# A hybrid decoder step on one core: its scales in column pieces, x transposed raw and kept for the residual

## The chip, the core and the metric

The kernel runs on one core of a Trainium2 chip. Its engines work side by side, each through its own instruction stream: TensorE (PE in the profile, its weight loads PEld), VectorE (DVE), ScalarE (ACT), GpSimd (POOL) and SyncE (SP), which here only issues transfers to the DMA engines. Matmuls write to PSUM (eight banks of 512 floats in each of 128 partitions), everything else lives in SBUF. The metric is the device time of one execution in microseconds (us).

## The reference

One inference step of a one-layer decoder trunk for a prompt of 512 positions and for 8 samples of one position, width 1024, float32. Cut to what the change touches:

```python
cs = jax.nn.silu(c)
mod = cs @ w_mod + b_mod
sh1, sc1, g1, sh2, sc2, g2 = jnp.split(mod, 6, axis=-1)
h = _rmsnorm(x, norm1_g) * (1.0 + sc1) + sh1
u = h @ w_in
qa, fa, ia, oga, xb, yb, ga, gb = _split_cols(u)
...
x = x + g1 * (merged @ w_out)
h2 = _rmsnorm(x, norm2_g) * (1.0 + sc2) + sh2
x = x + g2 * (jnp.square(jax.nn.relu(h2 @ w_ff1)) @ w_ff2)
y = _rmsnorm(x, final_norm_g)
```

Between the two parts stand a gated linear recurrence over eight heads (states, outputs) and a convolution with a second recurrence. `_rmsnorm` divides by the root of the mean square of a row of x.

## The kernel before, in words

All activations are kept transposed: 128 channels on the partitions, the 512 positions of the prompt and the 8 samples in the free dimension (T = 520, in two halves of 260). A product with a weight tile of 1024 x 128 goes over eight k blocks of 128 channels. For precision every weight tile and every activation is split into a high and a low part (`hi`, `lo`, type fp32r), so that one k block takes six matmuls of 260 columns: high with high, high with low, low with high, each for two halves. Weight tiles come through a pool of four buffers (`wst`); ACT makes their high parts, DVE their low parts. Outside the start, `gemm` (line 156) runs these products; their matmuls stand under L151.

**The start** (`begin`) prepares h and makes the first three products (the f, q and output-gate columns of head 0) by hand. There, PE, ACT and DVE instructions run in the order in which the code writes them: `InOrder` chains each instruction to the one before it on its engine. That helper is line 69, so all of them stand under L69 and are told apart by their tiles. In the order of before:

- SP loads the conditioning vectors, x in four tiles of 128 positions (`xn`), one weight tile, the eight row blocks of `w_mod` for the scales (part 1; 128 x 1024 each, tile `wm`), and three weight tiles; later eight row blocks for the shifts (part 0), and further weight tiles.
- ACT sums squares of x, DVE makes the inverse roots (`rs_y`), and ACT and DVE multiply x by them row by row, while positions are still on the partitions.
- PE multiplies the conditioning by the row blocks (`mod_rows`, tile `pt`) and between them transposes the normed x, block by block; ACT and DVE copy the blocks back (`put_back`).
- When all eight row blocks are through, `mod_out` copies the sums out (`modev`), and `mod_cols` transposes them into columns and adds bias and gain: `modT`, the scales.
- `scaled(k)`: ACT writes the high part of block k of x times its scale, DVE the low part. `products(n, ks)` makes tile n's products over blocks ks. The weight tiles' parts are `fhi` and `flo`.
- The products run without the shift. The shift rows follow; `mod_cols(0, ...)` gives `shp`. The shift's share in the first three products is added by matmuls of the shift with the raw weights (tile `pw`, then `shwh`, `shwl`) and an indicator of positions (`ind`). `again(k)` rewrites block k of h with the shift (ACT high part, DVE `ht` and low part, POOL the samples) for all later products.
- `masks_of`, `bounds`, `exponentials`, `indicator`, `decays` prepare small constants of the recurrences, mostly on DVE.

Behind the start come the heads, gates and branches, then **`load_xT`** (line 927): it reads x a second time, transposes it in 32 blocks through PSUM (`xin` to `pb`), with eight small transposes for the samples, and has ACT copy it into eight slots `ma`. These are the residual that `out_proj` adds to. The rest (the MLP in a Strassen-like scheme, the last norm) is not touched. The order outside the start is made by a scheduler from the dependencies and priorities.

Of the kernel before, what the change touches and what calls it, by code (L numbers as in the profile page):

```python
# [6 lines left out]
F32 = mybir.dt.float32  # L7
# [10 lines left out]
NB = 8  # L18
# [58 lines left out]
class Kernel:  # L77
# [204 lines left out]
    def bounds(self, r):  # L282

        nc = self.nc
        pl = self.hc.tile([128, 16], F32, name="pl")
        self.transpose_in(pl, r, 16)
# [45 lines left out]

    def parameters_mod_in(self, r):
        pm = self.consts.tile([128, 64], F32, name="pm")
        self.transpose_in(pm, r, 64)
        self.bmod, self.n1g, self.n2g = pm[:, 0:48], pm[:, 48:56], pm[:, 56:64]
        for part in (1, 4):
            c = self.bmod[:, part * 8:part * 8 + 8]
            self.nc.vector.tensor_scalar(c, c, 1.0, None, OP.add)
# [64 lines left out]
    def load_rows(self, part, k, t=None):  # L404

        t = t or self.start.tile([128, D], F32, name="wm", bufs=NWM)
        self.nc.sync.dma_start(t, self.i["w_mod"][0, k * 128:(k + 1) * 128, part * D:(part + 1) * D])
        return t

# [51 lines left out]
    def norm_samples(self):  # L461
        nc = self.nc
        j = self.pmm.tile([128, 2, 512], F32, name="mm").rearrange("p a b -> p (a b)")
        nc.vector.tensor_tensor(j[:NB], self.xsn, self.xsn, OP.mult)
        nc.vector.tensor_reduce(self.ss1[:NB, NC:NC + 1], j[:NB], mybir.AxisListType.X, OP.add)

    def norm_x(self):
        nc, ss = self.nc, self.ss1
        for t in range(NC):
            j = self.pmm.tile([128, 2, 512], F32, name="mm").rearrange("p a b -> p (a b)")  # L470
            last = nc.scalar.activation(j, self.xn[:, t], AF.Square, accum_out=ss[:, t:t + 1])
        ss = ss[:, 0:8]
        nc.vector.tensor_scalar(ss, ss, 1.0 / D, EPS, OP.mult, OP.add)
        self.rs1 = self.rsqrt_small(ss, 8)
        return last

    def scale_x(self):
        nc, ss = self.nc, self.rs1
        for t in range(NC):
            x = self.xn[:, t]  # L480
            if t % 2:
                nc.scalar.activation(x, x, AF.Copy, scale=ss[:, t:t + 1])
            else:
                nc.vector.tensor_scalar(x, x, ss[:, t:t + 1], None, OP.mult)
        nc.vector.tensor_scalar(self.xsn, self.xsn, ss[:NB, NC:NC + 1], None, OP.mult)

    def xcols(self, k, n=1):
        return self.xn[:, :, k * 128:(k + n) * 128]

    def transposed(self, k, n, ps):  # L490

        for j in range(n):
            x = self.xcols(k + j)
            for t in range(NC):
                self.nc.tensor.transpose(ps[:, j, t * 128:(t + 1) * 128], x[:, t], self.ident)
        return k, n, ps

    def put_back(self, copy, t):
        k, n, ps = t
        copy(self.xcols(k, n).rearrange("p t (j f) -> p j t f", j=n), ps.rearrange("p j (t f) -> p j t f", t=NC))  # L500

    def transposed_s(self):
        nc = self.nc
        ps = self.pps.tile([128, 512], F32, name="ps")
        for k in range(KO):
            nc.tensor.transpose(ps[:, k * NB:(k + 1) * NB], self.xsn[:, k * 128:(k + 1) * 128], self.ident[:NB, :NB])
        xs = self.start.tile([128, KO, NB], F32, name="xhs")
        nc.vector.tensor_copy(xs, ps[:, :KO * NB].rearrange("p (k b) -> p k b", b=NB))
        return xs

    def scaled(self, k, shift=False):


        nc = self.nc
        sc, sh = self.modc(1, k)[:, 0:1], self.shp[:, k, 0:1]
        v = lambda t: t[:, :L].rearrange("p (t f) -> p t f", f=128)
        (hi, lo), x = self.h[k], self.xcols(k)
        if not shift:
            nc.scalar.activation(v(hi), x, AF.Copy, scale=sc)
            return lambda: nc.vector.scalar_tensor_tensor(v(lo), x, sc, v(hi).bitcast(F32), OP.mult, OP.subtract)  # L520
        f = self.start.tile([128, L], F32, name="ht", bufs=2)
        self.start_act = nc.scalar.activation(v(hi), x, AF.Identity, bias=sh, scale=sc)
        nc.vector.tensor_scalar(v(f), x, sc, sh, OP.mult, OP.add)
# [403 lines left out]
    def load_xT(self):  # L927

        nc, i = self.nc, self.i
        xs = self.tail.tile([16, D], F32, name="rows", bufs=1)[:NB]  # L930
        nc.gpsimd.dma_start(xs, i["x_sample"][:, 0])
        pt = self.ppt.tile([128, 512], F32, name="pt")
        for k in range(KO):
            nc.tensor.transpose(pt[:, k * NB:(k + 1) * NB], xs[:, k * 128:(k + 1) * 128], self.ident[:NB, :NB])
        xst = self.tail.tile([128, KO * NB], F32, name="xst", bufs=1)
        nc.vector.tensor_copy(xst, pt[:, :KO * NB])
        self.x = []
        for m in range(KO):
            t4 = self.tail.tile([128, NC, 128], F32, name="xin", bufs=2)
            nc.gpsimd.dma_start(t4, i["x_prompt"][0].rearrange("(t p) f -> p t f", p=128)[:, :, m * 128:(m + 1) * 128])  # L940
            ps = self.ppb.tile([128, 512], F32, name="pb")
            for c in range(NC):
                nc.tensor.transpose(ps[:, c * 128:(c + 1) * 128], t4[:, c], self.ident)
            x = self.slot(self.ma, "ma")
            nc.scalar.copy(x[:, :L], ps)
            nc.vector.tensor_copy(x[:, L:], xst[:, m * NB:(m + 1) * NB])
            self.x.append(x)
# [617 lines left out]
    def run(self):  # L1565
# [17 lines left out]
        self.hlast = self.hc.tile([128, KO, 9], F32, name="hlast")  # L1583
        self.oaT_d = self.dram.tile([H, 128, L], F32, name="oaT_d")
# [67 lines left out]
    def begin(self):  # L1652
# [6 lines left out]
        ps = lambda: self.pps.tile([128, 512], F32, name="ps")  # L1659
        self.load_c()  # L1660
        self.identity()
        rb, rm, par = self.load_bounds(), self.parameters_mod(), self.parameters()
        rows = [self.start.tile([128, D], F32, name="wm", bufs=NWM) for _ in range(KO)]
        self.load_x()
        keys = [self.head_cols(0)[j] for j in (0, 1, 3)]
        raw = [self._load_w(keys[0], self.wst)]
        rows = [self.load_rows(1, k, t) for k, t in enumerate(rows)]
        raw += [self._load_w(key, self.wst) for key in keys[1:]]
# [11 lines left out]
        def samples(shift):  # L1680
# [3 lines left out]
            else:  # L1684
                q.tensor_tensor(fs, xs, self.modT[:, 8:16, 1:9], OP.mult)
                parts(slice(0, KO))
# [9 lines left out]
        self.norm_samples()  # L1696
        self.bounds(rb)
        self.parameters_mod_in(rm)
        self.masks_of(4)
        last = self.norm_x()  # L1700
        self.exponentials()
# [194 lines left out]
```

## Time and profile before

| what | value |
|---|---|
| median of 3 runs | 1022.83 us (1021.65 to 1023.39) |
| the profiled execution's own time | 1022.73 us |
| its span, first to last instruction | 1020.9 us |
| PE, DVE, ACT busy | 98%, 66%, 50% of the span |
| mean granted PE clock | 0.995 |
| HBM read, written | 123.61 MB, 11.26 MB |

The profile is of one execution. A row of the timeline gives the start in us, the busy time, the engine, the line, the operation, output and inputs, the shape and how many instructions were merged; in brackets the engine's idle time before it and what ended that. A row of a tile's view gives the least, median and greatest duration in ns. A row of the groups gives the busy time in us, the mean duration in ns, and the idle time before. A fp32 matmul leaves two records, so `x16` in the trace can be eight matmuls.

### The profile page before, as it was taken

The page shows a single profiled execution, that of the slowest core. Times are in us where ns is not written, and L with a number is a line of the kernel's source. Part 1 is how long each engine was busy: PE and PEld are TensorE (multiplying, and loading weights), DVE is VectorE, ACT ScalarE, POOL GpSimd, SP SyncE. Part 2 cuts the span into 40 slices and gives each one's busy share as a digit, 9 for nine tenths or more (in the row PEclk, how much of TensorE's full clock was granted, in tenths as well). Part 3 has the DMA queues.
Part 4 walks back from the last instruction along what each step waited for, and adds up shares of the span by engine and source line. Part 5 has one row for each costly group of instructions (what it writes and reads, how often), then busy time and mean ns, then how long its engine had stood idle before and what let it go on. Part 6 is the DMA issues. An engine that isn't in the chain of part 4 may idle for free. (4 is left out here: it accounts for less than half of the span.)

```text
span 1020.9 us, 23540 instructions
## 1 busy us (share of the span) xinstructions
PE 996.0 (98%) x9756; PEld 966.2 (95%) x9756; DVE 673.5 (66%) x1412; ACT 514.0 (50%) x964; POOL 123.9 (12%) x229
## 2 busy tenths in 40 slices
PE   5999999999999999999999999999999999999997
PEld 3899999999999989998999999999999999999997
DVE  6776867786596667345233557677766776777685
ACT  4555735645573564334211235466555655646663
POOL 3210000000000001001010001021321231242150
PEclk9999999999999999999999999999999999999998
DMA  9673353434335335239656677331672483273242
GB/s 322 220 210 109 107 169 102 122 117 143 114 108 157 115 108 168 76 116 298 195 163 191 201 218 217 85 99 46 149 182 64 97 194 104 53 170 89 63 83 84
DMA packets 201821, 143.67 MB, mean 141 GB/s; under 512 B 6766, under 2 KB 189702, under 8 KB 201706
## 3 DMA queue, kind: packets, MB, share of 16 engines
q1 hardware_dynamic: 191090, 128.08, 42.1%
q0 software_dynamic: 10608, 14.05, 7.1%
q8 instruction: 76, 1.25, 0.5%
q14 instruction: 31, 0.25, 0.1%
q10 hardware_dynamic: 16, 0.03, 0.0%
HBM read 123.61 MB, written 11.26 MB: 132 GB/s over the span
## 5 line engine op out<-in xcount | busy, mean ns | idle before, releaser
L151 PE MATMUL mm<-h,whi 128*128 128x260 f32 (+1 forms) x2944 | 488.8, 285 | 0.0
L151 PEld LDWEIGHTS mm<-h,whi 128*128 128x128 f32 x2944 | 409.7, 189 | 3.3 <-issue 2.5
L151 PE MATMUL mm<-h,wlo 128*128 128x260 f32 x1472 | 303.5, 285 | 0.0
L112 ACT CAST whi<-wst 128x1024 fp32r<-128x1024 f32 x164 | 171.8, 1049 | 229.8 <-PE mm L151 178.9
L115 DVE TENSOR_TENSOR wlo<-wst,whi 128x1024 fp32r<-128x1024 f32 x164 | 200.3, 1222 | 125.6 <-ACT whi L112 124.2
L151 PEld LDWEIGHTS mm<-h,wlo 128*128 128x128 f32 x1472 | 230.5, 189 | 0.8 <-issue 0.4
L151 PE MATMUL mm<-a,whi 128*128 128x260 f32 x512 | 84.0, 284 | 0.0
L151 PEld LDWEIGHTS mm<-a,whi 128*128 128x128 f32 x512 | 70.3, 188 | 1.7 <-ACT whi L112 1.2
L151 PE MATMUL mm<-a,wlo 128*128 128x260 f32 x256 | 52.2, 284 | 0.0
L893 POOL DMA_DIRECT2D t<-obT_d x8 | 4.4, 550 | 392.5 <-PE pb L798 302.6
L1286 DVE TENSOR_TENSOR f<-f 128x260 f32<-128x260 f32 x64 | 27.4, 427 | 27.6 <-ACT f L1281 26.9
L1275 ACT ACTIVATE ft<-ft,fsh 128x512 f32<-128x512 f32 (+2 forms) x36 | 24.0, 675 | 36.1 <-DVE ft L1272 36.1
L151 PE MATMUL mm<-b,whi 128*128 128x260 f32 x256 | 41.6, 285 | 0.0
L1278 POOL TENSOR_TENSOR ft<-ft,fsh 128x8 f32<-128x8 f32 x28 | 18.4, 658 | 186.9 <-DVE ft L1272 186.9
L151 PEld LDWEIGHTS mm<-a,wlo 128*128 128x128 f32 x256 | 39.6, 188 | 0.0
L151 PEld LDWEIGHTS mm<-b,whi 128*128 128x128 f32 x256 | 35.0, 188 | 2.1 <-ACT whi L112 1.2
L682 DVE TENSOR_TENSOR X<-X,tb 128x512 f32<-128x512 f32 x48 | 31.0, 687 | 3.2 <-PE ps L674 1.9
L1320 POOL DMA_DIRECT2D ma<-snap x28 | 28.0, 1014 | 35.8 <-issue 27.2
L1302 POOL DMA_DIRECT2D ma<-snap x28 | 26.0, 927 | 40.1 <-DMA ma<-snap 28.2
L1281 ACT ACTIVATE f<-ft 128x520 f32<-128x520 f32 (+1 forms) x36 | 20.8, 587 | 15.0 <-POOL ft L1279 13.0
L175 ACT ACTIVATE gate<-pb,pa 128x260 f32<-128x260 f32 x32 | 15.4, 482 | 21.0 <-PE pb L798 21.0
L151 PE MATMUL mm<-b,wlo 128*128 128x260 f32 x128 | 25.8, 283 | 0.0
(573 smaller groups left out, 1867.9 us busy)
## 6 DMA issues: line engine op xcount, KB each, us to landing
wst<-in_w_in_dram SPq DMA_DIRECT2D x64, 512.0 KB, 4.2
wst<-in_w_mod_dram SPq DMA_DIRECT2D x32, 512.0 KB, 4.6
wst<-in_w_ff_dram SPq DMA_DIRECT2D x64, 256.0 KB, 3.7
wst<-in_w_ff_dram SPq DMA_DIRECT2D x32, 512.0 KB, 4.6
wm<-in_w_mod_dram SPq DMA_DIRECT2D x16, 512.0 KB, 10.5
st<-in_state_hgrn_dram SPq DMA_DIRECT2D x8, 512.0 KB, 5.1
vb<-vd SPq DMA_DIRECT2D x8, 512.0 KB, 3.7
out_dram<-st SPq DMA_DIRECT2D x8, 512.0 KB, 3.5
```

The source lines that it names most:

```text
L112: ins = self.nc.scalar.copy(hi, st)
L115: self.nc.vector.tensor_tensor(lo, st, hi.bitcast(F32), OP.subtract)
L151: self.last_product = self.nc.tensor.matmul(ps[s][:, :c.stop - c.start], x, y[:, c], start=first and n == 0, stop=last and n == 2)
L175: ins = self.nc.scalar.activation(out, x, AF.Sigmoid, **kw)
L682: nc.vector.tensor_tensor(half, half, factors(tbs, x, b), OP.mult)
L893: nc.gpsimd.dma_start(t, self.obT_d[n])
L1275: nc.scalar.activation(t[:, :p], t[:, :p], AF.Relu, bias=sh[:, 0:1])
L1278: eng.tensor_tensor(t[:, p:], t[:, p:], sh[:, 1:9], OP.add)
L1281: nc.scalar.activation(f, self.two(self.ft)[:, a:a + n], AF.Square)
L1286: self.nc.vector.tensor_tensor(f[:, n], f[:, a], f[:, b], op)
L1302: nc.gpsimd.dma_start(x[1][:, b], v[:, :n], accum_op=OP.add)
L1320: nc.gpsimd.dma_start(x[t][:, a], s[p], accum_op=OP.add)
```

## The change

- **Scales in pieces of columns.** Instead of eight row blocks, `w_mod`'s part 1 is loaded as four pieces of 256 columns over all 1024 rows (1 MB each), each behind one of the first weight tiles. `piece` multiplies one piece by the conditioning, all eight k at once; `piece_cols` turns it into the scales of two blocks k. The shift rows come as four loads of two row blocks.
- **x transposed raw.** As each tile of x lands, PE transposes it into all eight PSUM banks; DVE and ACT copy halves into eight tiles `xT` (slots `ma`).
- **The factors per block.** `spread_root` writes the inverse roots on the diagonal of four matrices (`rsd`), and a product with ones spreads them over all partitions (`spread`, tile `pb`). `rooted(k)` on DVE multiplies block k of `xT` by it. The multiplication row by row and `put_back` are gone.
- **Stored for the residual.** POOL adds the samples to `xT`, SP stores the eight tiles to DRAM (`xT_d`), and `load_xT` becomes eight loads.
- **Another order.** Products run for pairs of blocks behind their piece; `bounds`, the masks 4, 8 and 16 and the parameters go behind the first pairs; `again` is called for six blocks, not three, ahead of the matmuls of the shift; the shift is added at the very end.

```diff
+        for n in range(4):
+            if n < FIRSTS:
+                raw.append(self._load_w(keys[n], self.wst))
+            w = self.start.tile([128, KO, 256], F32, name="wm", bufs=4)
+            c = D + 256 * n
+            nc.sync.dma_start(w, self.i["w_mod"][0, :, c:c + 256].rearrange("(k p) n -> p k n", p=128))
+            pieces.append(w)
...
+    def spread_root(self, ps, ps_s):
+        nc, rs, eye = self.nc, self.rs1, self.ident
+        one = self.ones_r.bitcast(F32)
+        d = self.start.tile([128, NC, 128], F32, name="rsd")
         for t in range(NC):
+            nc.vector.tensor_scalar(d[:, t], eye, rs[:, t:t + 1], None, OP.mult)
...
+    def piece(self, i, w):
+        nc = self.nc
+        pt = self.ppt.tile([128, 512], F32, name="pt")
         for k in range(KO):
+            j = 32 * (k % 4)
+            nc.tensor.matmul(pt[j:j + 32, :256], self.cT[:, k, :], w[:, k, :], start=k < 4, stop=k >= 4)
+        return i, pt, self.mod_out(pt)
...
+        for t in range(NC):
+            for k in range(KO):
+                nc.tensor.transpose(banks[k][:, t * 128:(t + 1) * 128], self.xn[:, t, k * 128:(k + 1) * 128], self.ident)
+            nc.scalar.activation(junk[:, t * D:(t + 1) * D], self.xn[:, t], AF.Square, accum_out=self.ss1[:, t:t + 1])
+            if t == 1:
+                half(dve, 0, *range(KO))
+        half(dve, 1, 5)
+        half(act, 1, 4, 6, 0)
+        self.norm_root()
...
+        p = self.piece(0, pieces[0])
+        spread = pb()
+        self.spread_root(spread, pr)
...
+        self.piece_cols(p)
...
+        rooted = lambda k: nc.vector.tensor_tensor(self.xr[:, k], self.xT[k][:, :L], spread, OP.mult)
+        rooted(0)
...
+        products(0, 0, 1)
+        half(act, 1, 2, 3)
+        for k in range(KO):
+            plain.sync.dma_start(self.xT_d[k], self.xT[k])
         split_first(1)
+        p = self.piece(1, pieces[1])
         split_rest(1)
...
         products(1, 0, 1)
+        self.piece_cols(p)
+        for k in (2, 3):
+            rooted(k)
+            self.scaled(k)()
+        samples(False, slice(2, 4))
         split_first(2)
+        products(0, 2, 3)
+        p = self.piece(2, pieces[2])
+        products(1, 2, 3)
+        self.piece_cols(p)
         split_rest(2)
+        for k in (4, 5):
+            rooted(k)
             self.scaled(k)()
...
+        dve(pl, ppl[:, :16])
+        self.parameters_in(*par)
+        p = self.piece(3, pieces[3])
+        self.first.append([ps()[:, :HALF], ps()[:, :HALF]])
...
+        products(2, 0, 1, 2, 3)
+        self.piece_cols(p)
...
-        again(0, 1, 2)
-        products(0, 6)
-        products(1, 6)
+        again(*range(0, 6))
...
     def load_xT(self):
-        xs = self.tail.tile([16, D], F32, name="rows", bufs=1)[:NB]
-        nc.gpsimd.dma_start(xs, i["x_sample"][:, 0])
...
+        self.x = [self.slot(self.ma, "ma") for _ in range(KO)]
+        for m, x in enumerate(self.x):
+            self.nc.gpsimd.dma_start(x, self.xT_d[m])
```

**PE, from the scales to the products of the first tiles.** Names: `pt<-wm,cT` is the conditioning times a part of `w_mod`, `pt<-pick,modev` and `pb<-ident,modev` make the columns, `mm<-h,fhi` and `mm<-h,flo` are products, `xn` is x before the transposition. Before:

```order
L69 MATMUL pt<-wm,cT 32x256 x12
L69 MATMUL ps<-ident,rb 128x57
L69 MATMUL ps<-ident,rc 128x64
L69 MATMUL ps<-ident,rd 128x96 x2
L69 MATMUL pb<-ident,modev 128x36 x2
L69 MATMUL ps<-ident,xn 128x128 x8
L69 MATMUL mm<-h,fhi 128x260 x4
L69 MATMUL mm<-h,flo 128x260 x2
```

Now, the same place in the changed program:

```order
L69 MATMUL pt<-pick,modev 128x9 x2
L69 MATMUL mm<-h,fhi 128x260 x8
L69 MATMUL mm<-h,flo 128x260 x4
L69 MATMUL pt<-wm,cT 32x256 x8
L69 MATMUL mm<-h,fhi 128x260 x8
L69 MATMUL mm<-h,flo 128x260 x4
L69 MATMUL pt<-pick,modev 128x9 x2
L69 MATMUL mm<-h,fhi 128x260 x8
L69 MATMUL mm<-h,flo 128x260 x4
L69 MATMUL pt<-wm,cT 32x256 x8
```

The columns were made once, ahead of all products; now they are made four times, and each time behind the products of the pair before.

**DVE, from one pair of blocks to the next in the changed program.** `xn<-ma,pb` is `rooted`, `modT` the scales, `h<-xn,modT,h` a low part of h, `flo` one of a weight tile, `pl` and `pa` copies of parameters. Before, the low parts stood in one run:

```order
L69 TENSOR_TENSOR modT<-modT,pm 128x2x4x9
L69 SCALAR_TENSOR_TENSOR h<-xn,modT,h 128x512 x2
L69 TENSOR_TENSOR flo<-wst,fhi 128x1024
L69 SCALAR_TENSOR_TENSOR h<-xn,modT,h 128x512
L69 TENSOR_TENSOR flo<-wst,fhi 128x1024
L69 SCALAR_TENSOR_TENSOR h<-xn,modT,h 128x512 x5
```

Now, for the blocks 4 and 5:

```order
L69 TENSOR_TENSOR modT<-pt,pm 128x18
L69 TENSOR_TENSOR modT<-modT,pm 128x18
L69 TENSOR_TENSOR flo<-wst,fhi 128x1024
L69 TENSOR_TENSOR xn<-ma,pb 128x512
L69 SCALAR_TENSOR_TENSOR h<-xn,modT,h 128x512
L69 TENSOR_TENSOR xn<-ma,pb 128x512
L69 SCALAR_TENSOR_TENSOR h<-xn,modT,h 128x512
L69 COPY pl<-ps 128x16
L69 COPY pa<-ps 128x313
```

The first `modT` reads the columns that PE makes; each `rooted` stands directly ahead of the low part of the same block, and the copies of the parameters stand behind both.

**DVE, around the low part of the shift's weights (`shwl`).** `shp` are the shift columns, each pair of `ht` and `h<-ht,h` is one `again`. Before:

```order
L69 TENSOR_TENSOR shp<-pb,pm 128x2x4x9
L69 TENSOR_SCALAR ht<-xn,modT,shp 128x512
L69 TENSOR_TENSOR h<-ht,h 128x512
L69 TENSOR_SCALAR ht<-xn,modT,shp 128x512
L69 TENSOR_TENSOR h<-ht,h 128x512
L69 TENSOR_SCALAR ht<-xn,modT,shp 128x512
L69 TENSOR_TENSOR h<-ht,h 128x512
L69 TENSOR_TENSOR shwl<-pt,shwh 128x384
```

Now:

```order
L69 TENSOR_TENSOR h<-ht,h 128x512
L69 TENSOR_SCALAR ht<-xn,modT,shp 128x512
L69 TENSOR_TENSOR h<-ht,h 128x512
L69 TENSOR_SCALAR ht<-xn,modT,shp 128x512
L69 TENSOR_TENSOR h<-ht,h 128x512
L69 TENSOR_TENSOR shwl<-pt,shwh 128x384
L69 TENSOR_SCALAR ht<-xn,modT,shp 128x512
```

Six pairs stand between `shp` and `shwl`, of which the rows show the last three low parts; before there were three.

More of the change, by code (lines that the diff above doesn't have):

```diff
@@ new lines, in begin @@
+        xsr, xs = (self.start.tile([128, KO, NB], F32, name=n) for n in ("xsr", "xhs"))
+        dve(xsr, px[:, :KO * NB].rearrange("p (k b) -> p k b", b=NB))
+        nc.vector.tensor_tensor(xs, xsr, pr[:, None, :NB].to_broadcast([128, KO, NB]), OP.mult)
+        half(act, 1, 1)
+        rest = [self.scaled(0)]
+        split_rest(0)
+        rest[0]()
+        rooted(1)
+        rest.append(self.scaled(1))
+        rest[1]()
+        samples(False, slice(0, 2))
+        for k in range(KO):
+            plain.gpsimd.tensor_copy(self.xT[k][:, L:], xsr[:, k])
@@ L1730, in products @@
+        rows = []
+        for k in range(0, KO, 2):
+            w = self.start.tile([128, 2, D], F32, name="wm", bufs=4)
+            nc.sync.dma_start(w, self.i["w_mod"][0, k * 128:(k + 2) * 128, :D].rearrange("(j p) n -> p j n", p=128))
+            rows += [w[:, 0], w[:, 1]]
+        self.first = [mm()[:, :, :HALF]]
+        acc = [[self.first[0][:, s] for s in range(2)]]
         def products(n, *ks):
@@ L1766, in begin @@
         self.decays()
[L1767 to L1771 removed]
+        products(2, 4, 5)
+        products(0, 6)
+        products(1, 6)
         def shifted(n):
```

231 lines of the change are left out of this document (84 added, 147 removed).

## The prediction

> **What bounds the kernel now.** I read the first part of the page first (busy time by engine), then the windows of TensorE (PE) over the whole span, then the timeline of the start.
>
> ```profile
> span 1020.9 us, 23540 instructions
> PE 996.0 (98%) x9756; PEld 966.2 (95%) x9756; DVE 673.5 (66%) x1412; ACT 514.0 (50%) x964; POOL 123.9 (12%) x229
> ...
> 0.00:20.00 20.00, 7.89 (x52) 1.00 0.91 320
> 20.00:40.00 20.00, 18.94 (x183) 1.00 0.99 335
> ```
>
> The windows' columns are the length, PE's busy time with its records, the granted clock, the busy share of the DMA engines and GB/s. PE is busy for 996.0 of 1020.9 us. Of the 24.9 us without it, 12.1 us lie in the first 20 us and 1.1 in the next 20. So PE's stream sets the end, and two things move the time: PE work that is taken out or put in, and the time at which the start hands over to the dense stream.
>
> ```profile
> 26.87 0.51 PE L69 MATMUL mm<-h,fhi 128*128 128x260 f32 x2 [0.50 <-ACT h L69]
> ...
> 53.72 0.28 PE L151 MATMUL pt<-h,whi 128*128 128x260 f32 x1
> ```
>
> The first product starts at 26.87 us. The first matmul behind the start (L151) issues at 53.72. From 26.87 on PE hardly waits: VectorE (DVE) and ScalarE (ACT) are behind it, but never so far that it stops. The mark to compare is therefore 53.72: where does that matmul issue after the change?
>
> **The late part.** `load_xT` loses its 40 transposes; eight loads remain.
>
> ```profile
> L943 PE MATMUL pb<-ident,xin x32: 270/272/329, 602.8 to 633.1; 128*128 128x128 f32 x32
> ...
> 605.77 0.66 PE L934 MATMUL pt<-ident,rows 8*128 8x8 f32 x8
> ...
> 606.77 0.49 PE L151 MATMUL mm<-a,whi 128*128 128x260 f32 x2
> ...
> 617.78 0.52 PE L151 MATMUL mm<-a,whi 128*128 128x260 f32 x3
> 618.14 0.60 PE L943 MATMUL pb<-ident,xin 128*128 128x128 f32 x4
> 618.50 0.37 PE L151 MATMUL mm<-a,whi 128*128 128x260 f32 x1
> 618.70 0.40 PE L151 MATMUL mm<-a,wlo 128*128 128x260 f32 x2
> ```
>
> Three products take 617.78 to 618.14: in the dense stream a product steps 0.12 us. Products stand on both sides of the transposes without a gap, so what they push apart is what they cost. Four of L943 take 618.14 to 618.50, and the product behind them steps 0.20 instead of 0.12: 0.44 us. L934 and four of L943 take 605.77 to 606.77: 1.0 us. Together 1.0 + 7 x 0.44 = 4.1 us: **-4.1**. The new loads sit on POOL's queue, in slots that the merges free some 5.8 us (48 products of 0.12) apart from the first output tile on; I cost them at nothing, because each is wanted only behind a whole 5.8 us tile. Without that cover a load costs its landing, about 5 us once.
>
> **The start, up to the first product.** Now x is transposed as it lands and the factors follow. The squares and the root chain stay, ahead of everything that needs the factors:
>
> ```profile
> 10.20 1.03 ACT L69 ACTIVATE mm<-xn 128x1024 f32<-128x1024 f32 x1 [0.43 <-DMA xn<-in_x_prompt_dram]
> ...
> 13.81 0.17 DVE L69 SCALAR_TENSOR_TENSOR rs_y<-rs_t,rs_y 128x8 f32<-128x8 f32 x1
> ...
> 18.04 0.23 DVE L69 TENSOR_SCALAR m<-xi 128x128 f32<-128x128 int32 x1
> ...
> 18.62 0.29 DVE L69 TENSOR_TENSOR mask<-m,lt 128x128 uint8<-128x128 f32 x1
> ...
> 24.95 0.48 DVE L69 COPY pa<-ps 128x313 f32<-128x313 f32 x1 [2.18 <-PE ps L69]
> ```
>
> The factors are ready at 13.98. On DVE follow a copy of 128x256 (estimated at 0.4, a little under the 0.48 of the 313-wide `pa` copy), four diagonals of 128x128 at 0.23 (the 18.04 row), a small one, three small operations of `pm` and the two that make the scales: about 3.0, so the first `rooted` starts at 17.0 and the first product at 18.6, eight us earlier than now. The scales' first piece does not hold this up: behind x, which is there at 10.2 (the wait of the 10.20 row), come 0.5 + 1.0 MB.
>
> ```profile
> 10.00:15.00 5.00, 1.64 (x13) 0.56 (x17) 4.14 (x21) 4.75 (x8) 0.99 (x2) 1.00 1.08 364
> ...
> 30.00:35.00 5.00, 5.00 (x44) 5.00 (x43) 4.04 (x6) 5.00 (x10) 0.00 (x0) 1.00 1.01 402
> ```
>
> At the 364 GB/s of the first of these windows that is 4.3 us, so 14.5.
>
> **The start, from there on.** Here the order decides. Each pair of k blocks now goes round: PE evaluates a piece, DVE turns it into scales, multiplies x by the root (new, eight times), waits for ACT's high part, makes the low part, does so again for the second k, and only then can PE finish that pair and reach the next piece. Durations:
>
> ```profile
> L553 DVE TENSOR_TENSOR X<-mm,X x8: 685/693/701, 59.8 to 348.2; 128x520 f32<-128x520 f32 x8
> ...
> L69 DVE SCALAR_TENSOR_TENSOR h<-xn,modT,h 128x512 fp32r<-128x512 f32 x8 | 5.7, 754 | 1.8 <-ACT h L69 1.7
> ...
> L69 DVE TENSOR_TENSOR flo<-wst,fhi 128x1024 fp32r<-128x1024 f32 x3 | 3.7, 1217 | 0.1
> ...
> 22.40 1.07 PE L69 MATMUL pt<-wm,cT 128*32 128x256 f32 x16
> ...
> 25.77 0.23 DVE L69 TENSOR_TENSOR modT<-modT,pm 128x72 f32<-128x72 f32 x1
> ...
> 26.85 1.47 DVE L69 SCALAR_TENSOR_TENSOR h<-xn,modT,h 128x512 fp32r<-128x512 f32 x2 [0.85 <-ACT h L69]
> ```
>
> The root's multiplication is not in this trace; the nearest is L553, the same kind with one operand from PSUM: 0.69 (half of it if it streamed faster, 1.2, as `flo` takes for 1024, above; I take 0.69 since operands and width agree). From DVE's end at 26.00 over ACT to DVE's next start at 26.85 is 0.85. So one k is 0.69 + 0.85 + 0.75 = 2.29 on DVE.
>
> - k 0 and 1: 0.69, two small ones at the 0.23 of the `modT` row, `flo` 1.22 (it covers ACT), 0.75, then 2.29: 17.0 to 22.4.
> - PE finishes 6 products (0.72), a piece (1.0), 12 products (1.44), its columns with the hops on both sides (estimated at 0.35): 3.5, to 25.9. DVE has one `flo` in it and otherwise waits.
> - k 2 and 3: scales 0.46 + 2 x 2.29 = 5.0, to 30.9. PE again 3.5, to 34.4.
> - k 4 and 5: 0.46 + `flo` 1.22 + 4.58, to 40.7; then the copies of `pl` and `pa`, 0.65, which sit behind these on DVE and free the two banks that the third tile needs. PE has nothing else and stands still from about 36 to 41.3. Then 24 products and the columns, 3.2, to 44.5.
> - k 6 and 7: 5.0, to 49.6. From here PE has its fill of products, but DVE is behind.
>
> What DVE has left before the shift, in its order:
>
> ```profile
> 36.23 0.49 DVE L69 TENSOR_SCALAR ind<-tc,ind_b 128x520 fp32r<-128x520 int32 x1
> ...
> 36.64 1.22 DVE L69 TENSOR_TENSOR wlo<-wst,whi 128x1024 fp32r<-128x1024 f32 x1
> ...
> 37.77 0.20 DVE L69 RECIPROCAL ptmp<-ptmp 128x8 f32<-128x8 f32 x1
> ...
> 41.77 0.17 DVE L69 TENSOR_SCALAR c8n<-ptmp 128x8 f32<-128x8 f32 x1
> ...
> 47.85 0.54 DVE L69 TENSOR_SCALAR ht<-xn,modT,shp 128x512 f32<-128x512 f32 x1
> ...
> 49.10 0.56 DVE L69 TENSOR_SCALAR ht<-xn,modT,shp 128x512 f32<-128x512 f32 x1
> ...
> 50.38 0.55 DVE L69 TENSOR_TENSOR shwl<-pt,shwh 128x384 fp32r<-128x384 f32 x1
> ```
>
> Bounds 0.7 (four small ones at the 0.17 of the `c8n` row), three masks of 0.87 (18.04 to 18.91), indicator 0.9 (0.49 and two small ones), `wlo` 1.22, `decays` 4.2 (37.77 to 41.94), the shift columns 0.25: 9.9, to 59.5. Before, five masks and the bounds lay ahead of the first product, where DVE had room; now three masks and the bounds lie here. Then `again` is issued for six k instead of three before `shwl`: 6 x 1.25 (47.85 to 49.10) and 0.3 for the first wait on ACT, to 67.3; `shwl` 0.55; ten more products, 1.2. PE's first L151 matmul issues at about 69.0 instead of 53.72: **+15.3**. The stall that left the first 27 us has turned into waits between 19 and 67; what is late next is `shwl`, then the whole dense stream.
>
> The DMAs: behind x stand four weight tiles (2.1 MB), four pieces (4.2), the eight new stores (2.1), which SP's queue has ahead of three of the four shift loads and of the next weight tiles, and the shift rows (4.2). That is 12.6 MB, 31 to 35 us at the 402 and 364 GB/s above: landed by 46, wanted at about 52. I cost the stores at nothing; that cover is 6 us wide.
>
> **The clock.** PE stands still several times for 2 to 5 us. The trace has one such place:
>
> ```profile
> 372.00:374.00 2.00, 1.12 (x38) 1.00 0.00 0
> 374.00:376.00 2.00, 0.45 (x30) 0.98 0.66 198
> 376.00:378.00 2.00, 1.99 (x9) 0.50 0.59 198
> 378.00:380.00 2.00, 2.00 (x14) 0.66 0.53 148
> ```
>
> After 4 us with 1.57 us of work (1.12 + 0.45) the granted clock is 0.50 and then 0.66: 2 x 0.50 + 2 x 0.34 = 1.7 us lost. After the change there are five such stretches (19 to 22, 26 to 30, 36 to 41, 56 to 59, 63 to 67), four of them with work behind them on which the end waits. The bounds are 0 (none counts) and 12 (every PE term between the DVE stages, 3.5 + 3.5 + 3.2 + 1.2, at half clock). Four times 1.7 would be 6.8, but the stretches have work in them; I take **+4**.
>
> The Trainium skill, "TensorE: Matmul & The Clock Gate", section "Part 1: The HAM clock gate", says that the clock falls to half after an idle window of about 3.4 us and comes back after one of sustained work. The 0.50 row agrees. By that rule taken strictly, only the stretches of 36 to 41 and 63 to 67 would surely count, and the term would be an estimated 3.4.
>
> **Sum.** The profiled execution took 1022.73 us, 1.8 over its span and 0.1 under the median shown. 1022.7 - 4.1 + 15.3 + 4 = **1038** us.
>
> **Rivals.**
> - *PE at half clock in all of the start.* The early rows speak for it, since little PE work lies between 12 and 41. The term is 12 and one window behind the start adds 1.7: 1022.7 + 11.2 + 13.7 = 1047.6.
> - *The rounds are shorter than I lay them out.* If the three PE rounds (3.5 + 3.5 + 3.2) lay beside DVE work, only DVE's own list would count: 1022.7 + 11.2 - 10.2 + 2 for the clock, 1026. Against it: DVE's order has the scales of the next pair ahead of its `rooted`.
> - *Faster.* If ACT's round trips (seven of 0.85) were hidden as well and no clock was lost, the start would end 6 us earlier again: 1018. Its mechanism is that DVE never waits from 17.0 on; it decides the sign from the point where the start's end falls below 57.8 (53.7 + 4.1). Against it: `rooted`, ACT and the low part stand directly behind each other, for one k at a time.
> - *The shift rows are late.* The stores take DMA time and PE reaches the rows at 52; at 300 GB/s they land at 52 too, and DVE is the later anyway until 59. From there each us costs one: about 1041.
> - *The change does not do what it says*: the order of both kernels shows that it does; what is left is an end within noise, 1023.
>
> **How the numbers follow.** Chances: forecast 0.50, half clock 0.22, shorter rounds 0.16, late rows 0.03, faster 0.07, no difference 0.02. The range reaches from 1024 (below the shorter rounds, between them and the faster case) to 1048 (half clock). Within 0.2%, 2 us, is about what this measurement cannot tell from none. Faster 0.07, within 0.02, slower 0.91.
>
> **What would show it.** Right: first product near 18.6; DVE waiting for ACT about 0.85 us in front of each low part; PE idle before the third tile's products for some 5 us; the first L151 matmul near 69 to 74; granted clock below 1 between 20 and 45; no L943 near 600. Wrong: an L151 matmul before 58, or PE waits put down to `wm` or `xT_d` transfers.

## The result, and the profile after

| | before | after |
|---|---|---|
| median, beside each other on one chip | 1022.67 us (4 runs) | 1045.84 us (1043.31 to 1046.97, 4 runs) |
| ratio to before | 1 | 1.0224, 95% interval 1.0201 to 1.0247 |
| the profiled execution, its span | 1022.73, 1020.9 us | 1043.31, 1041.5 us |
| first L151 matmul | 53.72 us | 78.88 us |
| from there to the end of the span | 967.2 us | 962.6 us |

The change makes the kernel 2.2% slower. In the profiled executions the start ends 25.2 us later, and 4.6 us of that come back behind it: 25.2 - 4.6 = 20.6, which is the difference of the spans. The profiled execution of after is the fastest of its four; the medians lie 23.2 apart.

First the page of after (busy time by engine; the granted clock of PE in 40 slices, in tenths):

```profile
span 1041.5 us, 23550 instructions
PE 1004.2 (96%) x9738; PEld 974.1 (94%) x9738; DVE 678.5 (65%) x1428; ACT 508.8 (49%) x960; POOL 126.6 (12%) x245
...
PEclk7789999999999999999999999999999999999998
```

PE's windows in its first 80 us (length, PE busy with its records, granted clock, DMA share, GB/s):

```profile
20.00:40.00 20.00, 12.74 (x84) 0.71 1.06 353
40.00:60.00 20.00, 15.69 (x134) 0.83 0.33 110
60.00:80.00 20.00, 11.66 (x138) 0.81 0.41 110
```

Before, the window from 20 to 40 had 18.94 us of PE work at clock 1.00. Now it has 12.74 at 0.71. Two things are lost there: PE stands still, and when it works it works more slowly. PE's waits in the first 90 us of after (total, times, longest) say for what it stands still:

```profile
PE mm L69 <- ACT h L69: 5.4, 3, 1.9
PE mm L69 <- DVE shwl L69: 4.3, 1, 4.3
PE ps L69 <- DVE pl L69: 4.3, 1, 4.3
...
PE pt L69 <- DVE shp L69: 2.4, 1, 2.4
PE mm L69 <- POOL h L1656: 1.8, 1, 1.8
PE pt L69 <- DMA wm<-in_w_mod_dram: 1.8, 1, 1.8
```

These are the rounds of the prediction: for h, for `pl` (the bank of the third tile), for `shp` and `shwl`. One wait is not in its layout, 1.8 us for the samples' part of h, which POOL makes. Of the transfers of `w_mod` the first piece held PE (`wm`, 1.8 us); none of the shift rows did. The timeline of PE in after shows where the waits stand and what runs behind them:

```profile
15.13 1.94 PE L69 MATMUL pt<-wm,cT 128*32 128x256 f32 x16 [1.81 <-DMA wm<-in_w_mod_dram]
17.00 2.08 PE L69 MATMUL pb<-rsd,ones_r 128*128 128x128 f32 x8
...
22.44 0.59 PE L69 MATMUL mm<-h,fhi 128*128 128x260 f32 x1 [1.89 <-ACT h L69]
...
46.92 4.01 PE L69 MATMUL ps<-h,fhi 128*128 128x260 f32 x16 [4.31 <-DVE pl L69]
...
76.55 0.80 PE L69 MATMUL mm<-ind,shwl 128*128 128x260 f32 x2 [4.34 <-DVE shwl L69]
...
78.88 0.42 PE L151 MATMUL pt<-h,whi 128*128 128x260 f32 x1
```

The 16 products behind the wait for `pl` take 4.01 us, 0.25 each, where a dense product stepped 0.12; the first L151 takes 0.42 instead of 0.28. Windows of 2 us of PE in after show the clock beside the work:

```profile
20.00:22.00 2.00, 0.55 (x3) 0.50 1.13 311
22.00:24.00 2.00, 0.59 (x1) 0.50 1.10 348
24.00:26.00 2.00, 1.13 (x4) 0.50 1.10 351
26.00:28.00 2.00, 2.00 (x13) 0.50 1.12 328
28.00:30.00 2.00, 2.00 (x25) 0.98 1.12 357
...
46.00:48.00 2.00, 1.07 (x4) 0.50 0.55 225
...
50.00:52.00 2.00, 2.00 (x11) 0.51 0.00 0
52.00:54.00 2.00, 2.00 (x19) 1.00 0.00 0
```

Behind most waits stand some us of full work at half clock: 26 to 28, 36 to 38, 46.9 to 52, and 76.5 to past 82. Not behind every one: around the wait for `shp`, from 64 to 68, PE worked 1.57 of 4 us and the clock stayed at 1.00, though the same 1.57 of 4 us lost it in before (372 to 376). DVE, which waits for PE's columns, in its own timeline of after (the scales, the first `ht`, the sixth, `shwl`):

```profile
20.65 0.18 DVE L69 TENSOR_TENSOR modT<-pt,pm 128x18 f32<-128x18 f32 x1 [4.40 <-PE pt L69]
...
31.01 0.18 DVE L69 TENSOR_TENSOR modT<-pt,pm 128x18 f32<-128x18 f32 x1 [3.10 <-PE pt L69]
...
40.98 0.18 DVE L69 TENSOR_TENSOR modT<-pt,pm 128x18 f32<-128x18 f32 x1 [5.30 <-PE pt L69]
...
52.87 0.18 DVE L69 TENSOR_TENSOR modT<-pt,pm 128x18 f32<-128x18 f32 x1 [5.60 <-PE pt L69]
...
66.95 0.55 DVE L69 TENSOR_SCALAR ht<-xn,modT,shp 128x512 f32<-128x512 f32 x1
...
73.45 1.78 DVE L69 TENSOR_SCALAR ht<-xn,modT,shp 128x512 f32<-128x512 f32 x1
...
75.94 0.55 DVE L69 TENSOR_TENSOR shwl<-pt,shwh 128x384 fp32r<-128x384 f32 x1
```

Four times DVE waits 3 to 6 us for PE, and in between PE waits for DVE or ACT: the two take turns.

### The profile page after: what moved, and what is told of

Its sections match the earlier page's. It is cut to its first block, busy times and chain, and to the rows that moved or that the text cites. A ratio compares the mean times of both kernels' runs of the same rounds, so it can differ in the third digit from the quotient of the medians.

```text
span 1041.5 us, 23550 instructions
## 1 busy us (share of the span) xinstructions
PE 1004.2 (96%) x9738; PEld 974.1 (94%) x9738; DVE 678.5 (65%) x1428; ACT 508.8 (49%) x960; POOL 126.6 (12%) x245
## 5 line engine op out<-in xcount | busy, mean ns | idle before, releaser
L151 PE MATMUL mm<-h,whi 128*128 128x260 f32 (+1 forms) x2944 | 487.7, 285 | 0.1
L151 PEld LDWEIGHTS mm<-h,whi 128*128 128x128 f32 x2944 | 409.9, 189 | 3.6 <-issue 2.5
L151 PE MATMUL mm<-h,wlo 128*128 128x260 f32 x1472 | 304.4, 286 | 0.0
L151 PEld LDWEIGHTS mm<-h,wlo 128*128 128x128 f32 x1472 | 230.6, 189 | 0.8 <-issue 0.4
L151 PE MATMUL mm<-a,whi 128*128 128x260 f32 x512 | 82.9, 284 | 0.0
L151 PEld LDWEIGHTS mm<-a,whi 128*128 128x128 f32 x512 | 69.9, 188 | 2.1 <-ACT whi L112 1.6
L151 PE MATMUL mm<-a,wlo 128*128 128x260 f32 x256 | 51.7, 283 | 0.0
L1235 POOL TENSOR_TENSOR ft<-ft,fsh 128x8 f32<-128x8 f32 x28 | 18.4, 656 | 206.8 <-DVE ft L1229 206.8
L151 PE MATMUL mm<-b,whi 128*128 128x260 f32 x256 | 41.6, 285 | 0.0
L151 PEld LDWEIGHTS mm<-a,wlo 128*128 128x128 f32 x256 | 39.5, 188 | 0.0
L151 PEld LDWEIGHTS mm<-b,whi 128*128 128x128 f32 x256 | 35.1, 188 | 2.1 <-ACT whi L112 2.1
L570 DVE SCALAR_TENSOR_TENSOR st<-vb,fkq,st 128x128 f32<-128x128 f32 x64 | 17.9, 347 | 13.2 <-DMA vb<-vd 13.2
L151 PE MATMUL mm<-b,wlo 128*128 128x260 f32 x128 | 25.8, 283 | 0.0
```

Of the source, the lines that this page charges most:

```text
L151: self.last_product = self.nc.tensor.matmul(ps[s][:, :c.stop - c.start], x, y[:, c], start=first and n == 0, stop=last and n == 2)
L570: nc.vector.scalar_tensor_tensor(st[:, b], vb[:, b], fkq[:, 1, b:b + 1], st[:, b], OP.mult, OP.add)
L1235: eng.tensor_tensor(t[:, p:], t[:, p:], sh[:, 1:9], OP.add)
```

## The experiments

Nine kernels were run. "L151" is the start of the first L151 matmul in the profiled execution, the mark of the prediction. The runs come in groups, each with its own runs of before beside it (median 1022.67 with after, 1021.60 with e1 to e4, 1022.12 with e5 to e8, 1022.09 with e9). "Over before" is the median less that of before in the same group; for after it is 23.2, and the text compares kernels by this column.

| kernel | median (range), runs | over before | ratio to before, 95% | L151 |
|---|---|---|---|---|
| e1: old `load_xT`, no stores | 1051.14 (1049.95 to 1056.69), 4 | 29.5 | 1.0302 (1.0263 to 1.0342) | 80.74 |
| e2: filler matmuls, first try | 1052.68 (1050.86 to 1054.87), 4 | 31.1 | 1.0305 (1.0280 to 1.0330) | 88.86 |
| e3: `again` for three blocks | 1039.09 (1037.94 to 1040.28), 4 | 17.5 | 1.0171 (1.0150 to 1.0193) | 73.37 |
| e4: `rooted` ahead of the columns | 1032.39 (1031.29 to 1034.44), 4 | 10.8 | 1.0108 (1.0086 to 1.0130) | 68.86 |
| e5: filler matmuls, other banks | 1040.48 (1039.51 to 1041.50), 4 | 18.4 | 1.0180 (1.0167 to 1.0193) | 70.26 |
| e6: e3 and e4 | 1030.60 (1029.45 to 1031.79), 4 | 8.5 | 1.0083 (1.0067 to 1.0098) | 65.17 |
| e7: e6, small work moved | 1027.95 (1022.82 to 1030.33), 10 | 5.8 | 1.0047 (1.0029 to 1.0064) | 58.75 |
| e8: e7, fillers at the start | 1026.69 (1024.37 to 1029.74), 6 | 4.6 | 1.0047 (1.0029 to 1.0064) | 59.78 |
| e9: e8, fillers in the products | 1023.45 (1020.64 to 1025.95), 11 | 1.4 | 1.0009 (0.9997 to 1.0022) | 58.53 |

**e1, the late part and the stores undone.**

```diff
-            plain.sync.dma_start(self.xT_d[k], self.xT[k])
...
-            self.nc.gpsimd.dma_start(x, self.xT_d[m])
...
+            nc.gpsimd.dma_start(t4, i["x_prompt"][0].rearrange("(t p) f -> p t f", p=128)[:, :, m * 128:(m + 1) * 128])
...
+            for c in range(NC):
+                nc.tensor.transpose(ps[:, c * 128:(c + 1) * 128], t4[:, c], self.ident)
```

> The changed kernel with the late part undone: load_xT reads and transposes x a second time as before, and the eight stores of xT are left out. My theory: the late part is worth 4.1 us of TensorE and the stores are hidden, so this is 4 us slower than the changed kernel (1045.84 median), about 1050, and the first L151 matmul stays at 79 us. Rival (the stores cost something at the start): it gets back more than 1 us of the start, L151 before 78, and is less than 3 us slower.

It is 6.4 us slower than after (5.3 by the bare medians), and its start does not end earlier (80.74 against 78.88). So the stored xT is worth 5 to 6 us, more than the 4.1 of the sum, and no delay of the start by the stores shows.

**e2, the clock held by filler matmuls.** 158 products of ones with a constant tile, whose output nobody reads, stand in PE's waits.

```diff
+        def fill(count, out):
+            for _ in range(count):
+                nc.tensor.matmul(out, self.ones_r, filler[:, :out.shape[-1]], start=True, stop=True)
...
+        fill(38, p[1][:, 288:])
         products(2, 0, 1, 2, 3)
```

> The changed kernel with 158 filler matmuls on constants (output read by nobody) put into TensorE's waits of the start; nothing else moves there. Clock theory: the granted clock stays near 1 from 12 to 80 us, the start loses its 8 to 10 us of half clock, first L151 matmul near 70, total near 1037. Rival (the excess over my layout comes from longer waits on VectorE and ScalarE, not from the clock): L151 stays at 77 or later and the total within 2 us of 1045.8, or above it by what fillers delay.

Up to 38 us the clock stayed at 1.00 and the scales of blocks 4 and 5 came 3.4 us earlier. Then the edit made waits of its own. One of PE's waits in e2, and then a row of its timeline:

```profile
PE pt L69 <- DVE shwl L69: 4.0, 1, 4.0
```

```profile
42.93 7.03 PE L69 MATMUL pt<-filler,ones_r 128*128 128x224 f32 x38 [3.69 <-ACT modev L69]
```

The fillers wrote to free columns of banks that ACT (`modev`) and later DVE (`shwl`) still had to read. They waited for that reader and came too late to fill the wait: by then the granted clock was 0.50 (42 to 48 us), and 38 of them took 7.03 us (0.185 each), with the products waiting behind them. This run says nothing of the total; e5 repeats it.

**e3, three blocks again.**

```diff
-        again(*range(0, 6))
+        again(0, 1, 2)
...
-        again(6, 7)
+        again(*range(3, KO))
```

> The changed kernel with three blocks of again ahead of the low part of the shift's weights, as before the change, and the other five behind. My theory: VectorE reaches shwl three blocks earlier, 3.8 us, and TensorE's 4.3 us wait shrinks to about 1; first L151 near 75, total 1041 to 1042. Rival (the blocks only move behind and are waited for there): total within 1 us of the changed kernel.

It is 5.7 us faster than after (6.75 by the bare medians). The wait for `shwl` fell from 4.3 to 1.2 us, and with it the half clock behind it was gone: the first L151 took 0.28 us. Behind it stands a new wait of 1.7 us in all for h.

**e4, the root's multiplication ahead of the columns.** Each pair's `rooted` is issued before the pair's `piece_cols`, so DVE does it while PE still has its round.

```diff
+        rooted(2)
+        rooted(3)
         self.piece_cols(p)
         for k in (2, 3):
-            rooted(k)
             self.scaled(k)()
```

> The changed kernel with the root's multiplication of blocks 2 to 7 put ahead of the columns of their piece on VectorE, so that it runs in VectorE's waits for TensorE. My theory (the rounds are serial): per round 1.4 us of rooted and most of one 0.8 us round trip leave the path, three rounds, 6 to 7 us; first L151 near 72 to 73, total near 1039. Rival (the start is bound by TensorE at its half clock or by VectorE's tail, not by the rounds): less than 2 us.

It is 12.4 us faster than after (13.45 by the bare medians), about twice what was expected for the DVE time alone. In the profiled executions L151 came 10.0 us earlier. PE's waits for `pl` and `shp`, in e4:

```profile
PE ps L69 <- DVE pl L69: 1.4, 1, 1.4
...
PE pt L69 <- DVE shp L69: 0.4, 1, 0.4
```

They were 4.3 and 2.4, and the waits for ACT's h fell from 5.4 to 3.2 in all. That is 7.1 us less waiting. With it the granted clock was 1.00 from 32 to 60 us, and half clock that is gone fits the other 2.9 of the 10.0.

**e5, the fillers again, in banks that nobody else reads meanwhile** (153 products, output read by nobody).

```diff
-        self.first = [mm()[:, :, :HALF]]
+        spare = mm()
+        self.first = [spare[:, :, :HALF]]
...
+        fill(34, spare[:, 0, 260:512], False)
         products(2, 0, 1, 2, 3)
```

> The changed kernel with 153 filler matmuls on constants in TensorE's waits again, now in banks that no other engine reads at that time, fewer where they came in the way, and some ahead of the shift's matmuls too. In the run before this one the clock stayed at 1 up to 38 us and VectorE reached the third round 3.4 us earlier, but later fillers waited for copies out of their bank. Clock theory: granted clock near 1 from 12 to 76 us, first L151 matmul at 69 to 71, total 1036 to 1038. Rival (the excess over the layout is waiting on VectorE and ScalarE): L151 at 77 or later, total 1044 or more.

DVE's timeline in e5:

```profile
18.49 0.18 DVE L69 TENSOR_TENSOR modT<-pt,pm 128x18 f32<-128x18 f32 x1 [2.38 <-PE pt L69]
...
27.94 0.18 DVE L69 TENSOR_TENSOR modT<-pt,pm 128x18 f32<-128x18 f32 x1 [2.18 <-PE pt L69]
...
36.72 0.18 DVE L69 TENSOR_TENSOR modT<-pt,pm 128x18 f32<-128x18 f32 x1 [4.12 <-PE pt L69]
...
46.55 0.18 DVE L69 TENSOR_TENSOR modT<-pt,pm 128x18 f32<-128x18 f32 x1 [3.54 <-PE pt L69]
...
60.62 0.55 DVE L69 TENSOR_SCALAR ht<-xn,modT,shp 128x512 f32<-128x512 f32 x1
...
67.10 0.54 DVE L69 TENSOR_SCALAR ht<-xn,modT,shp 128x512 f32<-128x512 f32 x1
...
68.35 0.55 DVE L69 TENSOR_TENSOR shwl<-pt,shwh 128x384 fp32r<-128x384 f32 x1
```

PE's windows of 12 us in e5:

```profile
12.00:24.00 12.00, 9.80 (x86) 1.00 1.12 329
...
72.00:84.00 12.00, 10.26 (x87) 1.00 0.57 153
```

The clock is 1.00 in every window of the start, and L151 issues at 70.26, 8.6 us earlier than in after and beside the 69.0 that the layout without the clock term gave. Apart from the fillers, DVE, ACT and PE do the same work there in the same order. What differs is the clock, and one thing more: the sixth `ht` takes 0.54 us instead of 1.78, which is 1.2 of the 8.6. The rest, some 7 us, shows the clock term at the hand-over. The total fell by 4.8 us (5.4 by the bare medians, 3.8 between the profiled executions), not by 8.6, and missed the expected 1036 to 1038, because PE now reaches the dense stream before ACT is ready for it. PE's windows in the 30 us behind L151, of after and then of e5, and the two waits in those of e5:

```profile
78.90:93.90 15.00, 15.00 (x113) 0.87 0.62 168
93.90:108.90 15.00, 14.89 (x124) 1.00 0.45 141
```

```profile
70.30:85.30 15.00, 13.26 (x111) 1.00 0.52 141
85.30:100.30 15.00, 12.28 (x103) 1.00 0.57 167
```

```profile
82.11 0.27 PE L579 MATMUL ps<-ident,ma 128*8 128x128 f32 x1 [1.74 <-ACT ma L556]
...
98.59 0.75 PE L151 MATMUL mm<-h,whi 128*128 128x260 f32 x4 [2.72 <-ACT xb L782]
```

After loses 1.95 us there to the clock (0.13 x 15) and 0.1 to waits; e5 loses nothing to the clock and 4.5 us to waits. From L151 to the end e5 takes 4.8 us more than after (967.4 against 962.6); these 30 us hold 2.4 of them.

**e6, both orders together.** The edits of e3 and e4.

> The changed kernel with both edits of order: rooted ahead of the columns of its piece, and three blocks of again ahead of shwl. Alone they gave 13.5 and 6.8 us. My theory (two separate places, rounds and shift): they add, total 1025 to 1026, first L151 near 63. Rival (both gains are partly one thing, the clock that comes back): total 1029 or more.

The rival's number came, 1030.60: e6 is 2.3 us below e4, though L151 issues 3.7 us earlier. Its reason did not: at the hand-over the two edits nearly add, 13.7 us against 5.5 and 10.0 alone. What is missing lies behind it. The stream behind it, in PE's timeline of e6, has waits for blocks of h that `again` had not yet rewritten, the longer of two:

```profile
71.07 0.39 PE L151 MATMUL pt<-h,whi 128*128 128x260 f32 x1 [1.18 <-DVE h L69]
```

**e7, small DVE work moved into the waits for PE.** The parameters' transposes and copies go behind the second piece's columns, one mask into each wait for the columns, the bounds into the second, and POOL's eight copies behind the first samples. Against e6:

```diff
         rooted(2)
         rooted(3)
+        self.masks_of(4)
         self.piece_cols(p)
...
+        dve(pl, ppl[:, :16])
+        self.parameters_in(*par)
...
         rooted(4)
         rooted(5)
+        self.masks_of(8)
+        self.bounds(pl)
         self.piece_cols(p)
```

> The run with both orders, and the small work moved into VectorE's and TensorE's waits: the parameters' transposes and copies behind the columns of piece 1, one mask in each round's wait, bounds in the second, and GpSimd's copies of the samples into xT behind the first samples' part of h instead of ahead of it. Theory: 1.4 us of wait for the copies, 1 to 2 us of wait for the samples and some of the clock come back: 3 to 5 us, total 1021 to 1023, which is the kernel before. Rival (nothing of that is on the path any more): within 1 us of the run with both orders.

The median, 1027.95, missed the expected 1021 to 1023, and the runs fall into two groups: three at 1022.8 to 1023.2 and seven at 1027.8 to 1030.3. The mean granted clock was 0.993 in each of the three and 0.986 to 0.990 in the seven; half a per cent of 1020 us is 5 us, about what lies between the groups. The profiled run is one of the three, so its L151 at 58.75 goes with 1023, not with the median.

**e8, 36 fillers around the first piece** (output read by nobody), in e7.

```diff
+        fill(14, px[:, 256:512])
         p = self.piece(0, pieces[0])
...
+        fill(22, spare[:, 0, 260:512], True)
         products(0, 0, 1)
```

> The run before it in this list with 36 filler matmuls on constants around the first piece (14 ahead of it, 22 behind its columns). Clock theory: the first piece, the spreading and the first products run at full clock, 2 to 4 us less, total 1018 to 1020, faster than the kernel before. Rival (the fillers only take the place of waits for the transfer and for VectorE): no difference over 1 us.

The fillers held the clock to 24 us, no further; the total did not change beyond its spread and missed the expected 1018 to 1020. PE's timeline in e8 at the first products, and then a window of 1 us behind them:

```profile
21.32 0.39 PE L69 MATMUL mm<-h,fhi 128*128 128x260 f32 x1 [0.59 <-POOL h L1656]
22.62 1.29 PE L69 MATMUL mm<-h,fhi 128*128 128x260 f32 x6 [0.91 <-ACT h L69]
```

```profile
25.00:26.00 1.00, 1.00 (x12) 0.50 1.09 345
```

Here two short waits inside the first products were enough to lose the clock behind them. In e5 they were one wait of 1.53 us at the same place, with as much work around it (2.47 us from 20 to 24, against 2.45 in e8), and the clock stayed at 1.00. The span of e8's profiled execution is 4.6 us longer than that of e7's profiled one (1025.8 against 1021.2), but L151 comes only 1.0 later: the rest was lost behind the start, part of it from 960 to 980 us, where PE worked 17.61 us at clock 0.92 in e8 and 19.14 at 1.00 in e7.

**e9, 42 more fillers in those waits** (the expectation counts 43; output read by nobody).

```diff
                     for s in range(2):
+                        if x is wh and part == 0 and gaps[0] and (k, s) != (ks[0], 0):
+                            fill(gaps[0 if s else 1], spare[:, 0, 260:512], False)
...
+        fill(10, spare[:, 0, 260:512], False)
         for n in range(FIRSTS):
             shifted(n)
```

> e8 plus 43 more matmuls whose output nobody reads, in the waits inside the first products (for the samples' part and for ACT's high parts, near 21, 22 and 30 us) and ahead of the shift's low part. In e8 the granted clock fell to 0.50 at 24 to 28 and again at 31 to 35, behind those waits, and the runs of e7 and e8 spread over 5 to 7 us. Theory (the clock is what remains): granted clock 1.00 from 12 to 58, the first L151 matmul at 56 to 57 (59.8 less 3.0 to 4.0 us of work at half clock), the median at 1021 to 1023.5 with a spread of at most 3 us. Rival (as in e6, work pulled ahead only waits for DVE and ACT behind the start): L151 earlier, but the median stays at 1026 to 1028. Second rival (the spread has another cause): clock 1.00, but the spread stays at 5 us or more.

PE's windows of e9:

```profile
12.00:24.00 12.00, 10.82 (x96) 1.00 1.12 328
24.00:36.00 12.00, 11.73 (x109) 1.00 1.09 366
```

The clock is 1.00 throughout and the median, 1023.45, is within the expected 1021 to 1023.5. L151 at 58.53 missed the expected 56 to 57, and the spread of 5.3 us missed the 3 (the 15 runs of before beside it spread over 3.9). The median is 4.5 us below that of e7, yet the profiles show no gain in the start: e7's profiled execution, one of its three shorter ones, had a clock of 0.57 from 16 to 28 us and reached L151 at 58.75, only 0.2 later. Where e7's seven longer runs lost their clock was not profiled, so it is not shown that the fillers of the start are what keeps e9 from losing it; e8 shows that part of the spread arises behind the start. Against before, 1.0009 (0.9997 to 1.0022) cannot be told from no change: the reordering, with the clock held, undoes the loss, but no version here beats before.

## Why the prediction was right, and where its sum was off

The sign and the mechanism were right, and 1045.84 lies in the range of 1024 to 1048; but it lies nearer to the rival with half clock in all of the start (1047.6) than to the 1038 forecast. That nearness is chance: the clock was at 1.00 in places, from 52 to 70 us above all, so what the rival describes did not happen. The stages of the layout, from one DVE row to the next, in us (the first is the 17.0 of the layout less the 0.3 from the scales to `rooted` in after):

| stage | predicted | after | e5, clock held |
|---|---|---|---|
| to the first scales | 16.7 | 20.65 | 18.49 |
| to the scales of 2 and 3 | 9.2 | 10.36 | 9.45 |
| to those of 4 and 5 | 8.5 | 9.97 | 8.78 |
| to those of 6 and 7 | 10.1 | 11.89 | 9.83 |
| to the first `ht` | 15.0 | 14.08 | 14.07 |
| to `shwl` | 7.8 | 8.99 | 7.73 |
| to the first L151 | 1.75 | 2.94 | 1.91 |
| sum | 69.0 | 78.88 | 70.26 |

- **The clock, "+4": too small at the hand-over.** The difference of the last two columns, without the stage to `shwl`, is 2.16 + 0.91 + 1.19 + 2.06 + 0.01 + 1.03 = 7.4 us; 1.95 follow behind L151. That is 9.3 instead of 4. The prediction took four drops at 1.7 us and then less, since "the stretches have work in them". That work did not help: with 0.55, 0.59 and 1.13 us of work in the 2-us windows from 20 on, the clock stayed at 0.50. And there was a stretch that it did not list, the wait for the first piece before 15.13, which put the spread of the root on half clock. The Trainium skill, "TensorE: Matmul & The Clock Gate", section "Part 1: The HAM clock gate", names an idle window of about 3.4 us as what drops the clock; here waits of 0.59 and 0.91 us on both sides of one matmul were enough in e8, while one of 1.53 us in e5 did not drop it.
- **Behind the mark: a term put at nothing.** At the end of the kernel a held clock was worth only 4.8 us (e5), near the +4. What the sum then lacks is seen without the clock term: 1022.7 - 4.1 + 15.3 = 1033.9 by the layout, 1039.51 in e5's profiled execution. L151 came 1.3 us later than laid out there, and 4.5 us of waits for ACT follow it. The prediction took everything behind its mark as dense, so an earlier or later L151 counted in full. In after, where L151 comes 8.6 us later, these waits are absent (0.1 us), so the two errors do not add up.
- **The start up to the first product, 18.6.** It came at 22.44. At full clock it would still have been later than laid out: in e5 the first scales come at 18.49, 1.8 us behind the layout. The layout let DVE's list set this point and left out PE's: the piece, the spread and the columns stand one behind the other (15.13, 17.00) and DVE waits 4.40 for them. The piece itself was ready at 15.13, not at 14.5, and PE waited 1.8 us for it, a small case of the `wm` wait that the prediction named as a sign of being wrong.
- **The rounds.** Confirmed. At full clock the three lengths between the scales agree with e5 within 0.3 us each; DVE's tail behind them was laid out 0.9 too long. That the sum of the stages, 69.0, lies so near e5's 70.26 is partly luck: the first stage was 1.8 too short. The rival of shorter rounds (1026) asked for a DVE that does not wait for the columns; it waited four times.
- **PE idle ahead of the third tile for some 5 us**: 4.31. **ACT ahead of each low part, 0.85**: 0.79.
- **Six `again`.** 8.99 instead of 7.8, and the 1.2 are one `ht` of 1.78 us (below). e3 shows the whole worth of this term: 5.7 us with its clock.
- **The shift rows and the stores.** No wait of PE for them in after, and e1 without the stores ends its start no earlier. Nothing here speaks against costing them at nothing.
- **The late part, -4.1.** Right in kind, too small: e1 lies 6.4 above after (5.3 by the bare medians) and 968.5 - 962.6 = 5.9 by the profiles from L151 on. Where the 1 to 2 us beyond 4.1 arise was not traced. The eight loads (median 5.4 us to land) held nobody: there is no wait for them in the trace.

Put together, against the forecast: clock +5.3, first scales +1.8, the long `ht` +1.2, DVE's tail -0.9, the other stages +0.4, and behind L151 -4.6 - 1.95 + 4.1 = -2.4. That is +5.4; the profiled execution was 1043.31, 5.3 above 1038. By the median the excess is 7.8.

## What to carry to other kernels

Cutting one wait for inputs into pieces gained nothing here while the consumer of piece n stood ahead of the producer of piece n+1 in some engine's order: e4, which moves six instructions ahead of that point, took off 12.4 us, though even with it no version here beat before. A wait of PE costs its own length and, where the granted clock falls behind it, part of that again: in e4 7.1 us less waiting brought L151 forward by 10.0. So cost the PE work behind a sparse stretch at half clock for the next 2 to 6 us, as here, and know that not every such stretch loses the clock. And a start that is made shorter is worth only as much as the engines behind it are ready: 8.6 us at the hand-over were 4.8 at the end.

## What the runs showed of the hardware

- **Sparse work can count as idleness for the clock.** In after, 2.27 us of work in the six us from 20 to 26 (0.55 + 0.59 + 1.13) kept the granted clock at 0.50; it was 0.98 only after two more us of dense work (26 to 28). The amount of work alone does not decide it: 1.57 of 4 us lost the clock in before (372 to 376) and kept it in after (64 to 68), and 2.45 of 4 us lost it in e8, 2.47 kept it in e5 (20 to 24 in both). Matmuls whose output nobody reads keep it at 1.00 (e5, e9).
- **One `ht` of 1.78 us.** The other seven took 0.54 to 0.56. POOL's timeline in after at that place:

```profile
73.53 0.52 POOL L1839 MEMSET fkq<- 128x96 f32 x4
73.99 0.96 POOL L1839 MEMSET at<- 128x1024 f32 x1
```

The long `ht` runs from 73.45 to 75.23, over the whole of these. In e1, e3, e4, e6 and e7 the `ht` that begins just ahead of these memsets is long too (1.78 to 1.80), and in before, where they come behind the last `ht`, none is. In e2, e8 and e9 an `ht` begins just as closely ahead of them (0.09 us) and takes only 0.65; there the four small memsets take 0.80 instead of 0.52. The Trainium skill, "SBUF — State Buffer", section "SBUF: two separate sides", says that GpSimd and VectorE, in a mode that uses both ports, share a pair of ports which one of them holds for a whole instruction, the first to start. That the two hold each other up agrees; that the first keeps the pair does not agree with the six long ones, as the `ht` began 0.08 to 0.09 us earlier by the trace and was the one held up (spans on POOL are rough). Why three kernels behave otherwise is open. No run was made to move the memsets, so the cause is argued, not shown.
- **The spread.** Runs of before lie within 4.5 us; those of e7 within 7.5, in two groups 5 us apart, with nothing changed between them. The mean granted clock goes with the groups (0.993 against 0.986 to 0.990), so one and the same program may or may not keep its clock. The places need not lie in the start: in before's profile the clock was lost near 376 us, in e8's near 970.
